# A causal mask moved from the matrix engine to the vector engine, in one attention step of a decoder block

## The chip, the core and the metric

The kernel runs on one core of one Trainium2 chip. The metric is the device time of one execution in microseconds (us); lower is better. The core's engines work from lists of their own: PE multiplies matrices (PEld is its loading of weights), DVE is the vector engine, ACT the scalar engine, POOL does a little, and SP issues transfers. Each engine takes its list strictly in order; semaphores make an instruction wait for other engines.

## What is computed

One decoder layer on 512 tokens of width 1024: a half-step SwiGLU, a mixer (attention with 8 heads of 64 in three branches, beside a state-space part), a second SwiGLU, an embedding gate and a norm. Of the attention only the row statistics of two branches matter here. Selection keeps all eight blocks of 64 keys and the window is 512, so both branches see every earlier key, and their scores are plain causal ones:

```python
s = jnp.einsum('bqghd,bsgd->bghqs', qc, k_w).astype(jnp.float32) * scale
p_win = masked_softmax(s, wmask)            # wmask: key position <= query position
...
def masked_softmax(s, mask):
    s = jnp.where(mask, s, NEG)             # NEG = -1e30
    m = jnp.max(s, axis=-1, keepdims=True)
    e = jnp.where(mask, jnp.exp(s - m), 0.0)
    return e / jnp.maximum(jnp.sum(e, axis=-1, keepdims=True), 1e-30)
```

## The kernel before

The two SwiGLU blocks and the projections are long rows of matrix products: fp32 values are split into a high and a low part (hi, lo), and each product is three matmuls. All matmuls are issued by the helper at line 133, so the profile tells them apart by tile names. The mixer lies in the middle of the run, between about 400 and 600 us.

In the mixer, queries are taken in four blocks of 128 rows (qb = 0 to 3). For every block, `scores(qb)` makes row scores with queries on the partitions and the first nk = 128(qb+1) keys along the free axis. Each step of its loop fills one bank of PSUM (`s_`, named ps_A, ps_B or ps_C by its tag; each tag has two banks that take turns): a matmul of QA with KA, one of QB with KB (the split parts), and a third matmul that adds the mask. That third one multiplies `identb`, an identity in bf16, by `maskq`, a 128x128 table of 0 and -1e30 in bf16, and accumulates onto the last 128 columns, where the diagonal is. Then DVE takes the row maximum (`nmax`, line 1261), and ACT the exponential with its row sum (line 918, in place in the bank). When the exponential has read the bank, the next score with that tag but one may start.

For qb = 2 and 3 a step holds one head and one branch (384 or 512 columns), so there are 16 steps for each of the two blocks, 32 in all. For qb = 0 and 1 a bank holds several heads, and there are 12 further steps.

The text `PLAN` (line 1590) gives the program order of the mixer's pieces: `t3` is a step of scores(3), `t2` of scores(2). Around them run the projections (ps_A from xh, xl with hi, lo), the state-space part (`s5_in`: DVE makes t, vv and z from ps_C; `s5_out`: PE multiplies u8 and z with so into ps_D), two gelu steps (lines 924 and 926 on DVE, with ACT between), the splits of the queries QA (line 1240) and the windows of the compressed branch (`windows`, line 1127: DVE adds cst, which a transfer brings, to pe and writes cs, cosr and sinr; a cst tile must be free of a gelu's `gt` before its transfer starts). The order on each engine is not the program order: line 1746 asks for a schedule by a simulated timeline when the program is built, so a change of one instruction can move others.

## Time and profile before

| | us |
|---|---|
| three runs: lowest, median, highest | 1045.18, 1047.27, 1047.62 |
| the profiled execution, its own time | 1044.96 |
| its span in the trace | 1043.2 |
| PE busy in the span | 1030.2 |
| DVE busy | 824.5 |
| ACT busy | 501.9 |

The profiled execution is 2.3 us below the median of the three runs; 1.8 us of its time lie outside the span. In a timeline row the first number is the start in the span, the second the duration; an "[idle before <-releaser]" at the end says how long the engine had been idle and what ended that. Durations of matmuls overlap, because the engine starts one before the last has drained; the step from one start to the next is what a matmul costs. Row groups ("x20") give busy time and the mean of one in ns.

### The profile page before, as it was taken

To read this page: it belongs to the slowest core of one execution; us is meant where nothing else is said; L and a number is where in the kernel's file an instruction comes from. 1 tells how busy PE (TensorE), PEld (TensorE's weight loads), DVE (VectorE), ACT (ScalarE), POOL (GpSimd) and SP (SyncE) were. 2 spreads that over 40 slices of the span, in tenths; PEclk is the share of its full clock that TensorE was granted. 3 is DMA by queue.
4 is the path that set the end of the run, shared out by engine and by line. 5 is a ranking of instruction groups with operands and counts; after the bars stand their busy time and mean duration, and the time that the engine had idled before them with its cause. 6 is when DMAs were issued, how large, how long until landed. Compare 5 with 4: busy or idle time off the path is not lost.

```text
span 1043.2 us, 15725 instructions
## 1 busy us (share of the span) xinstructions
PE 1030.2 (99%) x6057; PEld 875.7 (84%) x6057; DVE 824.5 (79%) x1382; ACT 501.9 (48%) x868; POOL 159.2 (15%) x180
## 2 busy tenths in 40 slices
PE   9999999999999999999999999999999999999997
PEld 6888888889889888776586688998899899899886
DVE  6798468988989766896688887996598588687666
ACT  6322232535336542476768855653365245245452
POOL 0003948207870200100000000000000000000001
PEclk9999999999999999999999999999999999999999
DMA  7434325636354748766410013433233333333412
GB/s 266 142 87 134 98 88 169 229 121 127 120 135 149 231 118 230 216 193 183 158 41 21 21 61 123 135 107 122 85 98 122 101 102 101 101 102 101 141 61 81
DMA packets 52394, 131.00 MB, mean 126 GB/s; under 512 B 10784, under 2 KB 19072, under 8 KB 52320
## 3 DMA queue, kind: packets, MB, share of 16 engines
q10 hardware_dynamic: 26352, 90.77, 27.3%
q0 software_dynamic: 5872, 17.93, 6.9%
q1 hardware_dynamic: 20096, 21.31, 6.5%
q8 instruction: 47, 0.77, 0.3%
q14 instruction: 27, 0.22, 0.1%
HBM read 114.09 MB, written 15.73 MB: 124 GB/s over the span
## 4 chain that ended last, share of the span: by engine, by line
PE 84%; DVE 5%; DMA 3%; POOL 3%; ACT 2%; issue 2%; SPq 0%; DVEq 0%; ACTq 0%; POOLq 0%
PE ps_A L133 25%; PE ps_C L133 24%; PE ps_B L133 20%; PE ps_D L133 15%; POOL ft L721 1%; POOL bt L720 1%; DMA kf<-kd 1%; DVE lo L166 1%; ACT e L918 1%; DMA kd<-r 1%; DVE el L1360 0%; DMA qf<-qd 0%; DMA h<-in_xT 0%; POOL ft L719 0%; POOL seen L559 0%
## 5 line engine op out<-in xcount | busy, mean ns | idle before, releaser
L164 ACT CAST hi<-raw 128x1024 fp32r<-128x1024 f32 (+2 forms) x143 | 144.4, 1010 | 250.3 <-PE ps_C L133 96.8
L133 PE MATMUL ps_C<-hq,hi 128*128 128x512 f32 x704 | 217.5, 390 | 0.2
L166 DVE TENSOR_TENSOR lo<-raw,hi 128x1024 fp32r<-128x1024 f32 (+2 forms) x143 | 174.2, 1219 | 40.6 <-ACT hi L164 39.9
L133 PEld LDWEIGHTS ps_C<-hq,hi 128*128 128x128 f32 x704 | 130.9, 188 | 28.1 <-DVE h L526 1.3
L133 PE MATMUL ps_C<-hq,lo 128*128 128x512 f32 x352 | 136.9, 389 | 0.0
L133 PE MATMUL ps_A<-xh,hi 128*128 128x512 f32 (+1 forms) x352 | 124.9, 355 | 0.5 <-ACT hi L164 0.5
L133 PE MATMUL ps_A<-xl,hi 128*128 128x512 f32 (+1 forms) x352 | 124.0, 352 | 0.1
L133 PE MATMUL ps_A<-xh,lo 128*128 128x512 f32 (+1 forms) x352 | 122.5, 351 | 0.2 <-DVE lo L166 0.2
L164 ACT CAST hi<-s 128x1024 fp32r<-128x1024 f32 x56 | 58.9, 1052 | 107.0 <-PE ps_D L133 60.9
L166 DVE TENSOR_TENSOR lo<-s,hi 128x1024 fp32r<-128x1024 f32 x56 | 70.7, 1262 | 19.9 <-ACT hi L164 19.7
L133 PEld LDWEIGHTS ps_C<-hq,lo 128*128 128x128 f32 x352 | 66.1, 188 | 13.8
L133 PEld LDWEIGHTS ps_A<-xh,hi 128*128 128x128 f32 x352 | 66.6, 189 | 10.2 <-ACT hi L164 0.7
L133 PEld LDWEIGHTS ps_A<-xh,lo 128*128 128x128 f32 x352 | 66.7, 189 | 9.5 <-DVE lo L166 0.6
L133 PEld LDWEIGHTS ps_A<-xl,hi 128*128 128x128 f32 x352 | 66.5, 189 | 9.7 <-DVE xl L192 0.8
L526 DVE SCALAR_TENSOR_TENSOR h<-ps_C,h 128x512 f32<-128x512 f32 x64 | 43.9, 687 | 36.6 <-PE ps_C L133 36.5
L133 PE MATMUL ps_B<-sh,lo 128*128 128x256 f32 x224 | 63.1, 282 | 0.3 <-DVE lo L166 0.3
L133 PE MATMUL ps_D<-sl,hi 128*128 128x256 f32 x224 | 63.1, 282 | 0.0
L133 PE MATMUL ps_B<-sh,hi 128*128 128x256 f32 x224 | 63.0, 281 | 0.0
L133 PE MATMUL ps_B<-sl,hi 128*128 128x256 f32 x224 | 62.9, 281 | 0.0
L133 PE MATMUL ps_D<-sh,hi 128*128 128x256 f32 x224 | 62.8, 280 | 0.0
L133 PE MATMUL ps_B<-xh,hi 128*128 128x512 f32 (+1 forms) x168 | 62.8, 374 | 0.0
L133 PE MATMUL ps_D<-sh,lo 128*128 128x256 f32 x224 | 62.6, 280 | 0.0
(440 smaller groups left out, 2474.4 us busy)
## 6 DMA issues: line engine op xcount, KB each, us to landing
raw<-in_wpack ACTq DMA_DIRECT2D x168, 512.0 KB, 3.5
si<-s5i POOLq DMA_DIRECT2D x8, 512.0 KB, 5.3
so<-s5o POOLq DMA_DIRECT2D x8, 512.0 KB, 5.6
h<-in_xT SPq DMA_DIRECT2D x8, 256.0 KB, 4.5
s5i<-fs POOLq DMA_DIRECT2D x1, 2048.0 KB, 11.5
xraw<-in_xT SPq DMA_DIRECT2D x8, 256.0 KB, 3.8
s5o<-gt POOLq DMA_DIRECT2D x1, 2048.0 KB, 13.4
s5i<-tcs POOLq DMA_DIRECT2D x2, 1024.0 KB, 10.4
```

Source lines behind the costliest of these rows:

```text
L133: return PE.matmul(o, lhsT, rhs, start=start, stop=stop, **kw)
L164: p, q = S.copy(hi[:, c], raw[:, c]), None
L166: q = V.tensor_tensor(lo[:, c], raw[:, c], hi[:, c].bitcast(F32), OP.subtract)
L526: V.scalar_tensor_tensor(h[:, m, :], o[m], 0.5, h[:, m, :], OP.mult, OP.add)
L720: G.tensor_tensor(bt, b2[:, 1], bc(psn[:, e]), OP.mult)
L721: G.tensor_tensor(ft[:, :, s_, :], ft[:, :, s_, :], bt, OP.add)
L918: S.activation(*args, **kw)
```

## The change

For the last two query blocks the third matmul goes. The matmul of QB with KB ends the accumulation, and DVE adds `maskq` (bf16) to the last 128 columns of the bank in place. For the first two blocks nothing changes.

```diff
-                    mm(s_[:, i], QB[0:112, h0 + i], KBg[0:112, g, rs, :nk], False, False)
-                mm(s_[:, :, :, nk - 128:], identb, maskq[:, None, None, :].to_broadcast([128, n, nb, 128]), False, True)
+                    mm(s_[:, i], QB[0:112, h0 + i], KBg[0:112, g, rs, :nk], False, qb > 1)
+                if qb > 1:
+                    V.tensor_tensor(s_[:, 0, 0, nk - 128:], s_[:, 0, 0, nk - 128:], maskq, OP.add)
+                else:
+                    mm(s_[:, :, :, nk - 128:], identb, maskq[:, None, None, :].to_broadcast([128, n, nb, 128]),
+                       False, True)
```

On PE 32 of the 44 mask matmuls go, with their weight loads; DVE gets 32 adds of 128x128. In the changed kernel the add has line 1260 and the maximum line 1265. The schedule also changes between the first score of qb = 3 and the first products of the attention's values, in the trace of before from 436 to about 555 us; outside that stretch the lists agree. Three places follow. A number behind a tile's name marks one buffer; "[waits Activation_49]" is a wait for ACT, DVE_49 for DVE, PE_49 for PE and DMA... for a transfer.

Place 1, PE, the third and fourth score of qb = 3 (ps_B_4315 and ps_B_4361). Before:

```order
L133 MATMUL ps_B_4315<-KA_3600,QA_4104 128x512 [waits Activation_49]
L133 MATMUL ps_B_4315<-KB_3601,QB_4105 128x512
L133 LDWEIGHTS identb_94
L133 MATMUL ps_B_4315<-maskq_3607,identb_94 128x128
L133 MATMUL ps_A_4327<-xh_3422,hi_4323 128x512
L133 MATMUL ps_A_4327<-xl_3423,hi_4323 128x512
L133 MATMUL ps_A_4327<-xh_3422,lo_4324 128x512
L133 MATMUL ps_B_4361<-KA_3600,QA_4104 128x512 [waits Activation_49]
```

PE in the changed kernel, the same two scores:

```order
L133 MATMUL ps_B_4315<-KA_3600,QA_4104 128x512 [waits PE_49,Activation_49]
L133 MATMUL ps_B_4315<-KB_3601,QB_4105 128x512
L133 MATMUL ps_A_4327<-xh_3422,hi_4323 128x512
L133 MATMUL ps_A_4327<-xl_3423,hi_4323 128x512
L133 MATMUL ps_A_4327<-xh_3422,lo_4324 128x512
L133 MATMUL ps_D_4368<-so_4192,u8_3639 64x128 [waits DMASW3_49,PE_49]
L133 MATMUL ps_D_4368<-so_4192,u8_3639 64x128
L133 MATMUL ps_D_4368<-so_4192,z_3640 64x128
L133 MATMUL ps_B_4361<-KA_3600,QA_4104 128x512 [waits Activation_49]
```

The masks are gone and three short products of the state-space part have come ahead of the fourth score. On ACT, not shown, the second exponential now stands behind a gelu's square (gt from yt), which was behind it before.

Place 2, DVE, ahead of the instruction that makes z_3641 for the state-space part. Before:

```order
L1261 TENSOR_REDUCE nmax_3644<-ps_B_4501 128x1 [waits PE_49]
L166 TENSOR_TENSOR lo_4617<-raw_4614,hi_4616 128x560 [waits Activation_49]
L1127 TENSOR_TENSOR cs_4654<-cst_4659,pe_3619 128x8x32 [waits DMAHW7_49,DMAHW6_49]
L1127 TENSOR_TENSOR cs_4655<-cst_4659,pe_3619 128x8x32
L990 SCALAR_TENSOR_TENSOR vv_4461<-r8_121,t1_4455 128x64 [waits DVE_49]
L990 SCALAR_TENSOR_TENSOR vv_4461<-r8_121,t1_4455 128x64 x3
L1261 TENSOR_REDUCE nmax_3644<-ps_B_4507 128x1 [waits PE_49]
L1261 TENSOR_REDUCE nmax_3644<-ps_C_4574 128x1 [waits PE_49]
L994 TENSOR_TENSOR z_3641<-vv_4461,si_4446 128x8x63 [waits DVE_49]
```

DVE in the changed kernel, up to the same z_3641:

```order
L1260 TENSOR_TENSOR ps_C_4574<-ps_C_4574,maskq_3607 128x128 [waits PE_49]
L1265 TENSOR_REDUCE nmax_3644<-ps_B_4501 128x1 [waits DVE_49]
L990 SCALAR_TENSOR_TENSOR vv_4461<-r8_121,t1_4455 128x64 [waits DVE_49]
L990 SCALAR_TENSOR_TENSOR vv_4461<-r8_121,t1_4455 128x64 x3
L1265 TENSOR_REDUCE nmax_3644<-ps_C_4574 128x1 [waits DVE_49]
L1240 SCALAR_TENSOR_TENSOR QA_4785<-qf_4788,QA_4785 64x512 [waits DMAHW1_49,Activation_49]
L1260 TENSOR_TENSOR ps_B_4507<-ps_B_4507,maskq_3607 128x128 [waits PE_49]
L924 SCALAR_TENSOR_TENSOR gt_4591<-gt_4591,yt_4438 128x512 [waits Activation_49]
L994 TENSOR_TENSOR z_3641<-vv_4461,si_4446 128x8x63 [waits DVE_49]
```

A query split (L1240) and a gelu step (L924) have come ahead of z, and eight adds stand ahead of it in all. PE's first product with z_3641 has moved back too: 20 more products of the value projection (ps_A, 280 wide) stand ahead of it than before.

Place 3, DVE, the second pair of cs, which needs a transfer into cst. Before:

```order
L1261 TENSOR_REDUCE nmax_3644<-ps_B_4537 128x1 [waits PE_49]
L926 SCALAR_TENSOR_TENSOR yt_4438<-gt_4591,yt_4438 128x512 [waits Activation_49]
L1108 SCALAR_TENSOR_TENSOR VL_3602<-ps_A_4620,ri_3686,VL_3602 128x4x64 [waits Activation_49]
L1110 TENSOR_SCALAR gp1_3606<-ps_A_4620,ri_3686 128x24
L1261 TENSOR_REDUCE nmax_3644<-ps_B_4585 128x1 [waits PE_49]
L1127 TENSOR_TENSOR cs_4654<-cst_4656,pe_3619 128x8x32 [waits DMAHW5_49,DMAHW4_49]
```

DVE in the changed kernel:

```order
L926 SCALAR_TENSOR_TENSOR yt_4438<-gt_4591,yt_4438 128x512 [waits Activation_49]
L1108 SCALAR_TENSOR_TENSOR VL_3602<-ps_A_4620,ri_3686,VL_3602 128x4x64 [waits Activation_49]
L1110 TENSOR_SCALAR gp1_3606<-ps_A_4620,ri_3686 128x24
L1240 SCALAR_TENSOR_TENSOR QA_4785<-qf_4818,QA_4785 64x512 [waits DMAHW7_49,Activation_49]
L1265 TENSOR_REDUCE nmax_3644<-ps_B_4531 128x1 [waits DVE_49]
L1260 TENSOR_TENSOR ps_B_4537<-ps_B_4537,maskq_3607 128x128 [waits PE_49,Activation_49]
L1127 TENSOR_TENSOR cs_4654<-cst_4656,pe_3619 128x8x32 [waits DMAHW3_49,DMAHW2_49]
L1127 TENSOR_TENSOR cs_4655<-cst_4656,pe_3619 128x8x32
L1265 TENSOR_REDUCE nmax_3644<-ps_B_4537 128x1 [waits DVE_49]
```

The maximum of score ps_B_4537 has moved from ahead of the gelu's last step (L926) to behind the pair that waits for the transfer. On SP that transfer now stands ahead of two transfers of queries that were ahead of it.

## The prediction

> **What bounds the kernel now.** I read the page's first part and the chain that ended last, then the stretches around the change, then PE's waits there.

> ```profile
> span 1043.2 us, 15725 instructions
> PE 1030.2 (99%) x6057; PEld 875.7 (84%) x6057; DVE 824.5 (79%) x1382; ACT 501.9 (48%) x868; POOL 159.2 (15%) x180
> PE 84%; DVE 5%; DMA 3%; POOL 3%; ACT 2%; issue 2%; SPq 0%; DVEq 0%; ACTq 0%; POOLq 0%
> ```

> PE sets the time: it idles only 13 us of the span. So a matmul taken away is worth its step, unless PE then waits. Whether it waits is read in the stretch of the 32 scores; columns are busy time (and count) of PE, PEld, DVE, ACT, POOL, then PE's clock, DMA share and GB/s:

> ```profile
> 434.00:442.00 8.00, 8.00 (x56) 5.82 (x55) 7.38 (x16) 3.70 (x7) 1.85 (x3) 1.00 0.76 225
> 442.00:470.00 28.00, 26.72 (x205) 20.14 (x203) 27.36 (x56) 20.98 (x45) 1.51 (x2) 1.00 0.64 199
> 470.00:484.00 14.00, 12.88 (x95) 10.15 (x95) 10.23 (x20) 10.84 (x26) 1.17 (x2) 1.00 0.46 113
> 484.00:524.00 40.00, 40.00 (x220) 24.77 (x216) 26.85 (x53) 26.84 (x71) 0.00 (x0) 1.00 0.54 181
> ```

> From 442 to 470 DVE is as full as PE (27.36 of 28 us against 26.72); from 470 on it has 3.8 us to spare, and from 484 another 13. The change takes work from the engine that bounds and gives it to one that for 28 us has no room. PE's waits from 430 to 525, and the masks:

> ```profile
> PE ps_B L133 <- ACT ps_B L918: 1.2, 1, 1.2
> PE ps_A L133 <- DVE cosr L1127: 0.7, 1, 0.7
> PE ps_A L133 <- PE ps_A L133: 0.4, 1, 0.4
> L133 PE MATMUL ps_B<-maskq,identb 128*128 128x128 bf16 x20 | 4.6, 231 | 0.0
> L133 PE MATMUL ps_C<-maskq,identb x12: 230/231/234, 460.5 to 521.7; 128*128 128x128 bf16 x12
> ```

> The first wait is for a score's exponential, the second for DVE's cosr. 20 and 12 masks of this form are the 32 that go.

> **Taken from PE.** A mask's 231 ns overlap its neighbours; its cost is in the steps between starts:

> ```profile
> 458.85 0.39 PE L133 MATMUL ps_B<-KA,QA 128*128 128x512 f32 x1
> 459.08 0.39 PE L133 MATMUL ps_B<-KB,QB 112*128 112x512 f32 x1
> 459.31 0.23 PE L133 MATMUL ps_B<-maskq,identb 128*128 128x128 bf16 x1
> 459.35 0.48 PE L133 MATMUL ps_C<-KA,QA 128*128 128x512 f32 x1
> 459.66 0.40 PE L133 MATMUL ps_B<-KA,QA 128*128 128x512 f32 x1
> ```

> Without a mask the step is 0.23 (458.85 to 459.08). With it, 459.31 to 459.66 holds the mask and one matmul: 0.35, so the mask costs 0.12. Bounds: 0.04, if only its own step (459.31 to 459.35) goes, and 0.23, if its whole duration goes. I take 0.12, since the longer step behind a mask recurs: 32 x 0.12 = 3.8 us. Against the span and the profiled 1044.96 this is the gross gain; ends 1.3 and 7.4.

> [...]

> **Given to DVE.** No add of 128 columns in PSUM is in the trace. The nearest rows are the same shape in SBUF, and 256 columns from PSUM:

> ```profile
> L660 DVE TENSOR_TENSOR u<-pi 128x128 f32<-128x128 f32 x1 | 0.3, 286 | 0.0
> L1280 DVE TENSOR_TENSOR ec<-ps_B,ec 128x256 f32<-128x256 f32 x4 | 1.7, 421 | 0.6 <-ACT ec L1279 0.6
> ```

> So 0.29, upper end 0.42. Durations overlap the next one a little:

> ```profile
> 441.79 0.68 DVE L1261 TENSOR_REDUCE nmax<-ps_B 128x1 f32<-128x512 f32 x1
> ...
> 455.25 0.42 DVE L984 TENSOR_TENSOR t<-ps_C,si 128x256 f32<-128x256 f32 x1
> 455.68 0.42 DVE L985 TENSOR_TENSOR t<-ps_C,si 64x256 f32<-64x256 f32 x1
> ...
> 466.42 0.68 DVE L1261 TENSOR_REDUCE nmax<-ps_C 128x1 f32<-128x512 f32 x1
> 467.02 0.68 DVE L994 TENSOR_TENSOR z<-vv,si 128x504 f32<-128x504 f32 x1
> ```

> A step of 0.60 for a duration of 0.68 where the next operation needs nothing of this one: an add takes 0.21 to 0.29 of the queue; I use 0.25, and 32 of them are 8 us. What matters is which PE wait they move. I counted DVE's new list forward from 441.79, the first maximum of before, with these steps: 0.60 to 0.70 for 512 columns, 0.43 for 256 (455.25 to 455.68).

> **Where the gain goes, up to cosr.** The first two masks stand ahead of a PE wait that ACT sets:

> ```profile
> 444.61 0.66 ACT L918 ACTIVATE ps_B<-ps_B,nmax 128x512 f32<-128x512 f32 x1
> 445.28 0.65 ACT L918 ACTIVATE ps_B<-ps_B,nmax 128x512 f32<-128x512 f32 x1
> 445.44 0.50 PE L133 MATMUL ps_B<-KA,QA 128*128 128x512 f32 x1 [1.18 <-ACT ps_B L918]
> 446.84 0.40 PE L133 MATMUL ps_B<-KA,QA 128*128 128x512 f32 x1
> 446.86 0.63 ACT L918 ACTIVATE gt<-yt 128x512 f32<-128x512 f32 x1 [0.81 <-DMA qd<-r]
> ```

> The third score starts 0.83 behind the first exponential (444.61 to 445.44), and ACT is what is late; 0.24 is lost. At place 1 the second exponential now stands behind the gelu's square, which waits for a transfer (446.86 in before; some 0.7 earlier now, because two adds, not two maxima, stand ahead of the sum that is transferred): it starts near 446.65 instead of 445.28, and the fourth score near 447.5 instead of 446.84. PE is there near 446.9: lost 0.6.

> The eighth score (ps_B_4507) waits for the fifth exponential, which in before came right behind its maximum:

> ```profile
> 456.57 0.69 DVE L1261 TENSOR_REDUCE nmax<-ps_B 128x1 f32<-128x512 f32 x1
> 457.36 0.66 ACT L918 ACTIVATE ps_B<-ps_B,nmax 128x512 f32<-128x512 f32 x1 [2.10 <-DVE nmax L1261]
> ```

> In the new DVE list that maximum has five adds ahead of it (1.25) and a query split, a gelu step, a scan and z that were behind it (4.2): it starts near 462.1, the exponential near 462.8, the score near 463.6, and PE is there near 462.3: lost 1.3.

> z_3641 itself comes 2.8 later (eight adds 2.0, split and gelu 1.3, a maximum fewer 0.6), near 469.8 instead of 467.02. In before PE waited a little for it:

> ```profile
> 467.24 0.29 PE L133 MATMUL ps_A<-hi,xl 128*128 128x280 f32 x1
> 467.36 0.29 PE L133 MATMUL ps_A<-hi,xh 128*128 128x280 f32 x1
> 467.75 0.44 PE L133 MATMUL ps_D<-so,z 128*64 128x128 f32 x4
> ```

> The 20 products that now stand ahead of it cover 20 x 0.12 (467.24 to 467.36) = 2.4, and PE itself is later by the losses (2.1) less ten masks (1.2): no wait, and the 0.25 of before is won.

> Next is the chain from the gelu's last step over two transfers into cst to cosr, on which the compression products wait (DVE, SP, PE):

> ```profile
> 473.53 0.69 DVE L926 SCALAR_TENSOR_TENSOR yt<-gt,yt 128x512 f32<-128x512 f32 x1
> 474.64 0.49 SPq L1120 DMA_DIRECT2D cst<-kcd  x1
> 478.13 1.12 DVE L1127 TENSOR_TENSOR cs<-cst,pe 128x256 f32<-128x256 f32 x2 [2.77 <-DMA cst<-kcd]
> 482.60 0.58 DVE L1127 TENSOR_TENSOR cosr<-cst,pe 128x256 f32<-128x256 f32 x1 [0.30 <-DMA cst<-vcd]
> 483.24 0.43 PE L133 MATMUL ps_A<-raw,cosr 128*64 128x256 f32 x1 [0.68 <-DVE cosr L1127]
> ```

> My count puts L926 at 473.1 in spite of ten adds, since the gelu's first step was brought forward, and SP no longer holds the transfer back behind the queries' (474.64 stands 0.4 behind L926's end). So cs starts near 477.3 and the cosr product near 482.4, 0.8 earlier. But two 384-wide scores (two steps of at most 0.23 each, so some 0.9 in all) that PE had done ahead of it now come behind. Net at this point: 0. The 17 masks gone by here (2.0 us) have paid for new waits. At place 3 one is plain: the maximum of ps_B_4537 stands behind cs, and the score that needs its bank behind that, so PE waits 1.4 there instead of 1.1 at two later places.

> **Behind cosr** 15 masks go, 15 x 0.12 = 1.8, beside a DVE with 13 us of slack; for the longer chain of each score (add, then maximum) and the new order up to 555 I take back 0.5. Sum: -1.3 us: profiled 1043.7 instead of 1044.96, and as the median of runs, which lies 2.3 above the profiled time, 1047.27 - 1.3 = 1046.0. A measurement of this kernel can tell about 0.3%, 3.1 us, from no change.

> **Rivals.** *All hidden:* PE's waits stay as they were, the gain is the gross 3.8 and the time 1043.4; with 0.16 a mask it is 5.1 and 1042.2. For it: the reordering puts 20 products ahead of z, and DVE is free from 470 on. Against: the full stretch 442 to 470.

> *Slower, by the turn of the score banks:* ps_B carries most scores of qb = 3, two banks in turn, and PE in its order stops at a score whose bank is not read. Each bank now passes an add and, in DVE's order, what stands between add and maximum. If each of nine scores from the fourth on waits 0.9 (between my 0.6 and 1.3), PE loses 8.1, nets +4.3 and ends at 1051.6. It decides for slower when new waits exceed 3.8 + 3.1 = 6.9. For it: the [2.10] above, where ACT already waited for a maximum; against: the scheduler moved other products ahead of the scores, and in before PE waited for a bank once. [...]

> *It thins nothing:* the new waits equal the gross gain over the whole stretch, not only up to cosr, and the time stays at 1047.3. This lies inside the forecast's range.

> **Numbers.** Chances: the forecast with its edge, so within 0.3%, 0.62; all hidden, faster by over 0.3%, 0.21; slower by over 0.3%, 0.17. The forecast's own range is 1044.2 to 1049.0 (add at 0.42 instead of 0.25: ten adds ahead of L926, +1.7; a mask at 0.04: +2.6). For 8 in 10 I go to 1042.5, the gross gain with dearer masks, and up to 1050.5, part of the slower case.

> **What would show it.** Right: 32 adds of 0.25 to 0.3 us at line 1260; PE's busy time down by 2 to 4 us and its idle time up by 2 or more between 442 and 484, on ACT's line 918; cosr's product starting 482 to 483; from 484 to 524 no new PE wait over 0.5. Wrong: if PE's waits from 442 to 484 stay at 2.3 (all hidden) or pass 7 (slower); if an add takes over 0.42; or if the lists up to 555 bring a wait I did not count.

## The result, and the profile after

The changed kernel takes 1054.3 us (median of 6 runs, 1052.92 to 1056.36) against 1046.8 of the kernel before (6 runs, 1045.18 to 1047.62): ratio 1.0073, 95% interval 1.0062 to 1.0084. It is slower by about 7.6 us, where 1046.0 with a range of 1042.5 to 1050.5 was forecast. Its profiled execution is the slowest of the six, so the profile shows some 2 us more than the median. One of the twelve runs of p3 below took 1448.4 us at a granted clock of 0.655, and p3's ratio is that of the other eleven.

The page of the changed kernel, first and fourth part:

```profile
span 1054.6 us, 15711 instructions
PE 1033.8 (98%) x6025; PEld 879.7 (83%) x6025; DVE 830.8 (79%) x1414; ACT 502.2 (48%) x868; POOL 159.5 (15%) x180
PE 82%; DVE 6%; DMA 4%; POOL 3%; issue 2%; ACT 2%; SPq 0%; DVEq 0%; ACTq 0%; POOLq 0%
```

PE has 32 matmuls fewer and is busy 3.6 us longer. The stretches say why; columns as before, the last but two is PE's granted clock:

```profile
434.00:442.00 8.00, 7.85 (x53) 5.82 (x52) 7.74 (x18) 3.97 (x8) 1.86 (x3) 1.00 0.74 221
442.00:470.00 28.00, 24.88 (x142) 19.11 (x140) 23.27 (x51) 16.68 (x34) 1.51 (x2) 0.82 0.51 161
470.00:484.00 14.00, 14.00 (x115) 12.04 (x116) 11.12 (x26) 9.40 (x23) 1.17 (x2) 1.00 0.67 165
484.00:524.00 40.00, 35.71 (x172) 21.13 (x170) 28.31 (x64) 25.88 (x63) 0.00 (x0) 0.96 0.57 178
524.00:560.00 36.00, 34.73 (x202) 29.08 (x200) 31.51 (x76) 24.29 (x81) 0.00 (x0) 1.00 0.16 47
```

From 434 to 560 PE idles 8.8 us, in the kernel before 2.6. Besides, its clock falls: 0.82 over 28 us and 0.96 over 40 are 5.0 and 1.6 us of full clock. DVE, which was full from 442 to 470 (27.36 of 28), is idle for 4.7 us there. PE's waits from 430 to 525 (total, times, longest):

```profile
PE ps_B L133 <- ACT ps_B L918: 3.3, 3, 2.2
PE ps_A L133 <- DMA raw<-in_wpack: 3.2, 2, 1.8
PE ps_A L133 <- DVE cosr L1127: 0.9, 1, 0.9
```

and the adds, from the view of the tile maskq (shortest, median and longest in ns):

```profile
L1260 DVE TENSOR_TENSOR ps_B<-ps_B,maskq x20: 277/292/300, 441.6 to 529.4; 128x128 f32<-128x128 f32 x20
L1260 DVE TENSOR_TENSOR ps_C<-ps_C,maskq x12: 277/288/300, 469.7 to 531.1; 128x128 f32<-128x128 f32 x12
```

An add takes 0.29 us, as forecast. Place 1, from the timeline of SP, ACT and PE:

```profile
443.35 0.33 SPq L1058 DMA_DIRECT2D qd<-r  x1
444.46 0.66 ACT L918 ACTIVATE ps_B<-ps_B,nmax 128x512 f32<-128x512 f32 x1
448.21 0.63 ACT L918 ACTIVATE gt<-yt 128x512 f32<-128x512 f32 x1 [2.96 <-DMA qd<-r]
448.74 0.64 ACT L918 ACTIVATE ps_B<-ps_B,nmax 128x512 f32<-128x512 f32 x1
449.56 0.50 PE L133 MATMUL ps_B<-KA,QA 128*128 128x512 f32 x1 [2.23 <-ACT ps_B L918]
```

The square stands between the exponentials, as the order said. But the transfer, issued 0.95 earlier than before (443.35, not 444.30), landed near 448.2 instead of 446.8, and the fourth score starts at 449.56. The clock behind it, by stretches of 4 us:

```profile
446.00:450.00 4.00, 1.77 (x12) 0.96 (x10) 1.43 (x5) 1.70 (x4) 0.00 (x0) 1.00 0.41 158
450.00:454.00 4.00, 4.00 (x32) 3.33 (x32) 3.89 (x9) 3.93 (x9) 0.76 (x1) 0.63 0.27 74
454.00:458.00 4.00, 4.00 (x20) 3.38 (x19) 3.94 (x7) 2.49 (x5) 0.00 (x0) 0.50 0.54 158
458.00:462.00 4.00, 4.00 (x12) 3.13 (x11) 3.85 (x10) 0.78 (x2) 0.00 (x0) 0.59 0.45 166
462.00:466.00 4.00, 4.00 (x28) 2.65 (x27) 2.35 (x7) 1.42 (x4) 0.75 (x1) 1.00 0.42 131
```

and two matmuls there, from the timeline:

```profile
457.50 0.63 PE L133 MATMUL ps_A<-xh,lo 128*128 128x512 f32 x1
457.92 0.63 PE L133 MATMUL ps_A<-xh,hi 128*128 128x512 f32 x1
```

After a stretch in which PE works 1.77 of 4 us the clock is at half for 10.2 us, and a 512-wide product takes a step of 0.42 instead of 0.23. Later on, from the timeline of DVE, SP, ACT and PE:

```profile
476.84 0.68 DVE L926 SCALAR_TENSOR_TENSOR yt<-gt,yt 128x512 f32<-128x512 f32 x1
477.59 0.47 SPq L1120 DMA_DIRECT2D cst<-kcd  x1
482.53 1.08 DVE L1127 TENSOR_TENSOR cs<-cst,pe 128x256 f32<-128x256 f32 x2 [1.88 <-DMA cst<-kcd]
487.62 0.43 PE L133 MATMUL ps_A<-raw,cosr 128*64 128x256 f32 x1 [0.88 <-DVE cosr L1127]
...
497.55 0.63 ACT L1238 ACTIVATE QA<-qf 128x512 fp32r<-128x512 f32 x1 [4.67 <-DMA qf<-qd]
499.64 0.43 PE L133 MATMUL ps_A<-raw,cs 128*63 128x256 f32 x1 [1.39 <-DMA raw<-in_wpack]
501.23 0.34 ACTq L107 DMA_DIRECT2D raw<-in_wpack  x1
504.92 0.67 PE L133 MATMUL ps_A<-yt,raw 128*128 128x512 f32 x1 [1.77 <-DMA raw<-in_wpack]
559.97 0.50 PE L133 MATMUL ps_D<-eh,VLc 128*128 128x512 f32 x1 [1.22 <-ACT eh L918]
```

cosr's product comes 4.4 us later than in the kernel before (483.24). Behind it ACT stands 4.67 us before a query copy, and the next weight loads in its queue (from 501.23) stand behind that. PE waits 1.77 us for the first of these and 1.22 us for eh, the high part of the attention's exponentials. Its wait of 1.39 us for raw at 499.64 is for a load that was issued ahead of that copy, by 491.7. So there are three suspects: the adds on DVE, single places of the new order (place 1 and its fallen clock, the loads), and the new order as a whole.

### The profile page after: what moved, and what is told of

Read it like the earlier page. It is cut to its first block, busy times and chain, and to the rows that moved or that the text cites. A ratio compares the mean times of both kernels' runs of the same rounds, so it can differ in the third digit from the quotient of the medians.

```text
span 1054.6 us, 15711 instructions
## 1 busy us (share of the span) xinstructions
PE 1033.8 (98%) x6025; PEld 879.7 (83%) x6025; DVE 830.8 (79%) x1414; ACT 502.2 (48%) x868; POOL 159.5 (15%) x180
## 4 chain that ended last, share of the span: by engine, by line
PE 82%; DVE 6%; DMA 4%; POOL 3%; issue 2%; ACT 2%; SPq 0%; DVEq 0%; ACTq 0%; POOLq 0%
PE ps_A L133 24%; PE ps_C L133 23%; PE ps_B L133 19%; PE ps_D L133 15%; DMA qf<-qd 1%; POOL ft L721 1%; DVE lo L166 1%; POOL bt L720 1%; DMA qd<-r 1%; DMA raw<-in_wpack 1%; DVE el L1364 1%; DMA cst<-kcd 0%; DVE s L342 0%; POOL ft L719 0%; DVE nmax L1265 0%
## 5 line engine op out<-in xcount | busy, mean ns | idle before, releaser
L133 PE MATMUL ps_C<-hq,hi 128*128 128x512 f32 x704 | 217.6, 391 | 0.4 <-DVE h L526 0.2
L133 PEld LDWEIGHTS ps_C<-hq,hi 128*128 128x128 f32 x704 | 130.8, 188 | 28.5 <-DVE h L526 1.9
L133 PE MATMUL ps_C<-hq,lo 128*128 128x512 f32 x352 | 136.8, 389 | 0.0
L133 PE MATMUL ps_A<-xh,hi 128*128 128x512 f32 (+1 forms) x352 | 125.2, 356 | 1.1 <-ACT xh L191 0.7
L133 PE MATMUL ps_A<-xl,hi 128*128 128x512 f32 (+1 forms) x352 | 124.8, 355 | 0.3 <-DVE xl L192 0.3
L133 PE MATMUL ps_A<-xh,lo 128*128 128x512 f32 (+1 forms) x352 | 123.2, 353 | 0.2 <-DVE lo L166 0.2
L133 PEld LDWEIGHTS ps_C<-hq,lo 128*128 128x128 f32 x352 | 66.1, 188 | 13.9
L133 PEld LDWEIGHTS ps_A<-xh,hi 128*128 128x128 f32 x352 | 67.0, 190 | 11.3 <-ACT xh L191 1.2
L133 PEld LDWEIGHTS ps_A<-xh,lo 128*128 128x128 f32 x352 | 67.1, 191 | 9.7 <-DVE lo L166 0.6
L133 PEld LDWEIGHTS ps_A<-xl,hi 128*128 128x128 f32 x352 | 67.0, 190 | 9.8 <-DVE xl L192 0.6
L133 PE MATMUL ps_B<-sh,lo 128*128 128x256 f32 x224 | 63.1, 282 | 0.3 <-DVE lo L166 0.3
L133 PE MATMUL ps_D<-sl,hi 128*128 128x256 f32 x224 | 63.1, 282 | 0.0
L133 PE MATMUL ps_B<-sh,hi 128*128 128x256 f32 x224 | 63.0, 281 | 0.0
L133 PE MATMUL ps_B<-sl,hi 128*128 128x256 f32 x224 | 62.9, 281 | 0.0
L133 PE MATMUL ps_D<-sh,hi 128*128 128x256 f32 x224 | 62.8, 280 | 0.0
L133 PE MATMUL ps_B<-xh,hi 128*128 128x512 f32 (+1 forms) x168 | 62.7, 374 | 0.0
L133 PE MATMUL ps_D<-sh,lo 128*128 128x256 f32 x224 | 62.6, 280 | 0.0
```

Source lines behind the costliest of these rows:

```text
L133: return PE.matmul(o, lhsT, rhs, start=start, stop=stop, **kw)
```

## Experiments

All ratios are to the kernel before on the same chip, with 95% interval; 0.1% is 1.05 us.

**Parts of the change.** The add for one block alone, no mask at all (the mask of qb = 2 and 3 is left out), and products with adds of zeros beside them. In these four the scheduler makes its own order each time.

```diff
-  False, qb > 1)  /  if qb > 1: V.tensor_tensor(...)
+  False, qb == 2) /  if qb == 2: V.tensor_tensor(...)    # e3; e4: qb == 3
-  V.tensor_tensor(s_..., maskq, OP.add)
+  pass                                                   # e5
+  if qb > 1: V.tensor_tensor(s_..., zero..., OP.add)     # e6, in the kernel before
```

> The add for the 16 scores of qb = 2, the mask product kept for the 16 of qb = 3. ACT has its two exponentials ahead of the gelu's square, as before. Theory A: no loss at place 1, ratio 0.997 to 1.001 (16 masks of 0.12 are 1.9 us of gain at most). Theory B, by the number of adds: half the loss, ratio 1.003 to 1.005.

> The add for the 16 scores of qb = 3, the product kept for qb = 2. ACT has the gelu's square between the first and the second exponential, as in the changed kernel. Theory A: nearly the whole loss, ratio 1.005 to 1.009, with a PE wait of 2 to 4 us for the second exponential and a clock below 0.9 from 442 to 470. Theory B, by the number of adds: half, ratio 1.003 to 1.005; by where DVE is full (442 to 470): also nearly the whole loss, but as many waits of about 1 us, at a clock of 1.00.

> No mask at all for qb = 2 and 3: neither product nor add. ACT's order at place 1 is that of before. All theories: the gross gain of the 32 products, 32 x 0.12 = 3.8 us, ratio 0.9963; by 0.081 each 2.6 us, 0.9975. Theory B: that with DVE as free as before nothing of it is lost. If it comes out at 1.000 or above, then taking the products away brings nothing even without the adds, because PE waits there for something else.

> The kernel before, mask products kept, with an add of zeros on VectorE of the same shape behind each of the 32: PE's work as before, DVE's and the scores' chain as in the changed kernel. ACT has the gelu's square between the first two exponentials, as in the changed kernel. If what costs is the adds on DVE (their time and the order that they make): the whole loss and no gain, ratio 1.007 to 1.012, with a clock drop behind place 1. If what costs is that PE has less work and so arrives early: ratio 1.000 to 1.004, since PE's work is that of before.

Measured: e3 1.0010 (1.0001 to 1.0020), e4 1.0068 (1.0051 to 1.0085), e5 0.9995 (0.9984 to 1.0007), e6 1.0062 (1.0043 to 1.0081). The loss goes with the 16 adds of qb = 3 and with the order in which the square splits the exponentials (e4, e6). It doesn't need PE's lighter work (e6). And leaving the products out, with nothing in their place, brought nothing clear of noise (e5). Adds and order still go together in all four.

**Place 1 undone, three ways.** e1 makes the first square issue behind the second exponential. e8 and e9 give the gelu other buffers, so that it does not wait for the transfer.

```diff
+  with tc.issue_after(exps[1]): act(t, x, AF.Square)     # e1, first gelu only
-GT = "r1", "r2"
+GT = "r3", "r2"                                          # e8;  e9: "rb1", "r3"
```

> All 32 adds stay; only the first gelu square is made to issue behind the second exponential of the qb = 3 scores, as it did in the kernel before. Theory A (the loss is that one order on ACT: a 3 to 4 us PE wait, the granted clock that falls behind it, and what comes late after it): PE is busy over 25.5 of 28 us from 442 to 470, the clock of that stretch is 0.97 or more, and the time comes back by 5 to 9 us, ratio to the kernel before 0.997 to 1.002. Theory B (DVE's 8 us of adds and the longer turn of each score bank): the wait only moves, ratio 1.005 to 1.009. Theory C (ACT's weight loads that come late at 498 to 506 us): half is left, ratio 1.002 to 1.005, and PE still waits over 2 us for raw.

> The changed kernel, with the first gelu's gt in the buffer tag r3 instead of r1, so that its square does not wait for the transfer qd<-r. ACT now has the square ahead of both exponentials, which follow each other. If the wait on the transfer is what costs: PE waits for exponentials 1.5 us or less at place 1, no clock drop from 448 to 462, ratio 1.000 to 1.004; if the adds on DVE cost wherever the square stands: 1.005 to 1.009.

> As the last, with both gelu tags changed (rb1 and r3), so that no gelu shares a buffer with what is transferred. ACT has the two exponentials first, then the square. Place 1 as in the kernel before; what is left is the load on DVE and the later waits (cosr, raw): ratio 1.000 to 1.005. Above 1.005 the wait on the transfer was not needed for the loss.

Measured: e1 1.0044 (1.0028 to 1.0060), e8 1.0042 (1.0029 to 1.0054), e9 1.0045 (1.0032 to 1.0059). About 3 us of 7.6 come back each time. In e8 cosr's product is at 483.15, as early as in the kernel before, and the loss lies behind it, where PE waits for loads among other things:

```profile
494.73 0.43 PE L133 MATMUL ps_A<-raw,cs 128*63 128x256 f32 x1 [1.01 <-DMA raw<-in_wpack]
500.27 4.94 PE L133 MATMUL ps_A<-yt,raw 128*128 128x512 f32 x7 [1.83 <-DMA raw<-in_wpack]
```

My first theory, that place 1 is the loss, was then too narrow, and it had been tested with edits that re-ordered the rest.

**The clock.** e7 fills the wait at place 1 with useless products.

```diff
+  [mm(o[0:64], KAc[:, 128:192], nm.xh[:, k, :], False, False) for _ in range(9)]   # kc, last k
```

> The changed kernel, with nine products more by a block of zeros (64 columns of KAc that stay zero, x 512, 0.23 us each, 2.1 us) in the kc projection, which stand on PE just ahead of the fourth score, in its wait of 2.2 us; ACT's order at place 1 stays. They do no useful work, so that PE is busy where it waited, and nothing comes earlier. If the fallen clock behind the wait is what costs there (4.8 us of clock time from 451 to 462): PE's wait for the second exponential under 0.5, clock 1.00 from 448 to 462, and faster than the changed kernel by 3 to 5 us, ratio 1.002 to 1.004 to the kernel before. If the wait alone costs, and the clock only shows it: no change or slower, ratio 1.007 to 1.010.

Measured: 1.0073 (1.0061 to 1.0086), no change. The filler did what it should, by stretches:

```profile
446.00:450.00 4.00, 3.32 (x14) 1.80 (x12) 1.53 (x6) 1.87 (x5) 0.00 (x0) 1.00 0.25 97
450.00:454.00 4.00, 3.30 (x37) 2.57 (x36) 3.92 (x8) 2.67 (x7) 0.76 (x1) 1.00 0.36 80
```

and by PE's timeline:

```profile
445.78 2.23 PE L133 MATMUL ps_A<-xh,KAc 128*64 128x512 f32 x9
449.39 0.50 PE L133 MATMUL ps_B<-KA,QA 128*128 128x512 f32 x1 [0.68 <-ACT ps_B L918]
470.35 0.44 PE L133 MATMUL ps_D<-so,u 128*64 128x128 f32 x4 [1.37 <-ACT yt L1023]
```

The clock stays at 1.00 through the whole stretch of e7's profile, and PE, faster there, waits at other places instead (1.37 for yt, 10.7 us of idle time from 430 to 620 against 9.5). My expectation of 3 to 5 us was wrong. But the scheduler re-ordered the stretch in e7 too (PE's list and DVE's differ from those of the changed kernel far beyond the filler), so e7 alone does not show what the fallen clock costs. The loss does not need it, though: p4 below, whose profile has one fall of 3.4 us (1.7 us of full clock), loses 10.9 us.

**The loads.** raw from GpSimd's queue: in the changed kernel (e10), with e8's buffer (e11), in the kernel before (e12), and with the add for qb = 3 alone (e13).

```diff
-  raw = unit(True, at=next(at["cmp"]))        # and "glu"
+  raw = unit(True, q=G, at=next(at["cmp"]))
```

> The changed kernel, with the weights of the compression and of the gated unit (raw) loaded from GpSimd's queue instead of ACT's, where they stand behind a copy that waits 4.7 us for the queries (qf<-qd). The scheduler then puts the two exponentials ahead of the gelu's square again. If that wait on ACT's queue is the second cause: PE waits for raw under 0.5 in 484 to 524 (3.2 in the changed kernel), ratio 1.002 to 1.005. If the adds on DVE cost all by themselves, ratio 1.005 to 1.009 and the wait is for something else.

> Both: raw from GpSimd's queue, and the first gelu's gt in r3, so that no square waits for qd<-r. If the two blocked waits on ACT are all of the loss, ratio 0.997 to 1.001; if the adds on a full DVE are a part of it that no order takes away, 1.002 to 1.004.

> The kernel before, mask products kept, with raw from GpSimd's queue. No PE wait for raw stands in its profile: no change, ratio 0.999 to 1.001. It is the measure for the last two.

> As the run with both, but the add for qb = 3 alone and the product kept for qb = 2. If the adds of qb = 3, which lie where DVE is full (442 to 484), are what costs: the same ratio as with all 32 adds, within 0.1%, or above. If each add costs alike: half of it. PE's wait of 1.2 for eh near 555 should be gone, as in the run with the add for qb = 3 alone.

Measured: e10 1.0101 (1.0080 to 1.0122), e11 1.0048 (1.0032 to 1.0064), e12 1.0048 (1.0033 to 1.0063), e13 1.0044 (1.0026 to 1.0061). The measure itself moved: e12, which differs from the kernel before by the queue of these loads and the order that the scheduler then makes, is 5 us slower. Like the kernel before it has no wait for raw, but PE's waits from 430 to 525 are these:

```profile
PE ps_B L133 <- ACT ps_B L918: 3.6, 3, 2.1
PE ps_D L133 <- ACT yt L1023: 1.6, 1, 1.6
PE ps_A L133 <- DVE cosr L1127: 0.5, 1, 0.5
```

So these four say nothing on the loads, but they gave the next theory: a re-ordered stretch can cost 5 us and more, whatever re-orders it.

**Work and order apart.** In the next kernels every engine's order is fixed by a table. p1 is the changed kernel in the order of the kernel before: the products left out of PE's list, each add right ahead of its maximum. p2 has no mask (left out, as in e5) and p3 products and adds of zeros, both in that order. p4 is the kernel before in the order of the changed kernel.

```diff
     block_kernel(tc, aps, out)
+    pin(tc)    # for each engine, each instruction of ORDER behind the one ahead of it, no wait
```

> The changed kernel's instructions in the order of the kernel before on every engine: its 32 products left out of PE's list, each add right ahead of its maximum in DVE's; ACT, GpSimd and SP word for word as before. If the new order is what costs: ratio 0.997 to 1.001, gelu's square behind both exponentials, PE's wait for cosr 0.7 to 3, clock 1.00. If the adds themselves cost (DVE full from 442 to 470, ten adds of 0.20 to 0.25 us ahead of cosr): cosr's product 2 us later than in the kernel before and ratio 1.002 to 1.006.

> No mask for qb = 2 and 3, neither product nor add, in the order of the kernel before. The pure worth of the 32 products: 3.8 us at 0.12 each, ratio 0.9963, or 2.6 us at 0.081, 0.9975; less where PE only waits more (cosr and the exponential, up to 2 us): 0.998 to 0.999. In the scheduler's own order it was 0.9995.

> Products kept, and an add of zeros of the same shape ahead of each of the 32 maxima, in the order of the kernel before. The pure price of the adds on DVE: if the order is what costs, ratio 1.000 to 1.002; if DVE's time is (32 x 0.20 to 0.25 us, 6.4 to 8), 1.003 to 1.008. In the scheduler's own order it was 1.0062.

> The kernel before, products and no adds, in the order of the changed kernel on every engine (each product right behind its score's second one). The pure price of the order: if it is the order, ratio 1.004 to 1.009, with the square of the gelu between the exponentials, its wait for qd<-r and a clock drop; if it is the adds, 0.999 to 1.003.

| work | old order | new order |
|---|---|---|
| products (before) | 1 | p4: 1.0104 (1.0087 to 1.0121) |
| adds (the change) | p1: 1.0015 (1.0004 to 1.0026) | 1.0073 (1.0062 to 1.0084) |
| neither | p2: 0.9988 (0.9979 to 0.9997) | |
| both | p3: 1.0025 (1.0016 to 1.0034) | |

This settles whether it is the work or the order. With the order kept, the change costs 1.6 us; the other 6.1 of its 7.6 come with the new order (1.0073 against 1.0015; the steps are rounded). With the work kept, the new order costs 10.9 us, and in that order the adds are 3.2 us better than the products (1.0073 against 1.0104). p1, p3 and p4 came out a little above the ranges that I had given for an order that costs all (1.001, 1.002 and 1.009 at most). No run has the table on a kernel's own order, with nothing changed; p5 below is the changed kernel with its own order in the table but for one step, and its 1.0071, against 1.0073, shows no price of the table itself. The stretches of p1, p2 and p4, in this order, three rows each:

```profile
442.00:470.00 28.00, 24.64 (x183) 19.40 (x182) 27.20 (x60) 19.04 (x41) 1.51 (x2) 1.00 0.58 195
470.00:484.00 14.00, 12.13 (x90) 9.97 (x88) 11.27 (x24) 10.85 (x26) 1.17 (x2) 1.00 0.48 118
484.00:524.00 40.00, 38.72 (x190) 23.96 (x191) 31.23 (x68) 26.55 (x68) 0.00 (x0) 0.96 0.59 190
```

```profile
442.00:470.00 28.00, 25.59 (x191) 20.21 (x189) 26.40 (x55) 20.15 (x42) 1.51 (x2) 1.00 0.62 204
470.00:484.00 14.00, 12.75 (x89) 10.33 (x87) 10.22 (x19) 11.69 (x30) 1.17 (x2) 1.00 0.50 119
484.00:524.00 40.00, 39.15 (x209) 25.53 (x209) 28.10 (x55) 26.79 (x71) 0.00 (x0) 1.00 0.57 185
```

```profile
442.00:470.00 28.00, 25.62 (x186) 19.07 (x185) 23.59 (x50) 17.62 (x36) 1.51 (x2) 1.00 0.58 177
470.00:484.00 14.00, 12.40 (x96) 9.99 (x95) 10.12 (x21) 8.84 (x24) 1.17 (x2) 1.00 0.60 157
484.00:524.00 40.00, 34.88 (x173) 19.88 (x174) 23.68 (x44) 24.91 (x62) 0.00 (x0) 0.96 0.56 177
```

PE's idle time in these rows is 2.4 us in the kernel before, 4.5 in p2, 6.5 in p1 and 9.1 in p4. p2 shows what the products are worth: over the whole span PE is busy 3.2 us less than in the kernel before (1027.0 against 1030.2). In these rows 2.1 us of new waits eat most of that, and by the ratio 1.25 are left (0.3 to 2.2 by its interval). In p4 no add is on DVE, which is idle for 4.4 us from 442 to 470, and PE waits 8.2 us for exponentials (up to 4.1 for one) all the same.

**Which place of the new order.** p5 is the changed kernel in its own order but for the second exponential, ahead of the square; p6 also has two loads ahead of the query copy on which ACT stands.

```diff
 ACT's list:
-exp 1, square, exp 2 ...   QA<-qf, ... raw, ... raw
+exp 1, exp 2, square ...   QA<-qf, ... raw, ... raw      # p5
+exp 1, exp 2, square ...   raw, raw, QA<-qf, ...         # p6
```

> The changed kernel in its own order on every engine, but for one step on ACT: the second exponential ahead of the gelu's square at place 1. If place 1 carries most of the price: PE's fourth score starts 2 to 3 us earlier, the clock stays at 1.00 from 448 to 462, and 3 to 6 us come back, ratio 1.002 to 1.0045. If PE then only waits elsewhere: 1.006 to 1.008.

> As the last, and two loads of raw weights on ACT's queue ahead of the query copy (QA<-qf) that waits 4.7 us for its transfer. If those loads carry the rest: PE's waits for raw fall from 3.2 to under 1.5 us and another 1 to 3 us come back, ratio 1.000 to 1.003. If the next wait takes its place (a score's exponential, or cosr): the same ratio as the last within 0.1%.

Measured: p5 1.0071 (1.0057 to 1.0085), p6 1.0079 (1.0065 to 1.0093). Neither gives anything back. Both steps do what they should: in p5 the fourth score starts at 447.44, in p6 no PE wait for raw is left. The next wait takes the place each time; PE's timeline of p5:

```profile
447.44 0.50 PE L133 MATMUL ps_B<-KA,QA 128*128 128x512 f32 x1
484.90 0.50 PE L133 MATMUL ps_B<-KA,QA 128*128 128x512 f32 x1 [2.21 <-ACT ps_B L918]
```

and of p6:

```profile
501.36 0.69 PE L133 MATMUL ps_B<-KA,QA 128*128 128x384 f32 x1 [2.80 <-ACT ps_B L918]
```

cosr's product stays at 487.30 and 486.89 (487.62 in the changed kernel). So no one of the places that I named carries the price of the order.

Two products tell in which part of the stretch it lies: cosr's first, and the first of the attention's values (eh with VLc). The first row is the kernel before (cosr's is at 483.24 there), the other two are p1:

```profile
549.66 0.39 PE L133 MATMUL ps_D<-eh,VLc 128*128 128x512 f32 x1
487.04 0.69 PE L133 MATMUL ps_A<-raw,cosr 128*64 128x256 f32 x1 [1.06 <-DVE cosr L1127]
553.54 0.39 PE L133 MATMUL ps_D<-eh,VLc 128*128 128x512 f32 x1
```

From the one to the other it is 66.4 us in the kernel before and 66.5 in p1 and p3, but 72.4 in the changed kernel, 74.3 in p4, 71.6 in p5 and 72.8 in p6. PE idles at most 0.1 us there in the old order and 4.1 to 5.4 in the new one, which also has two scores more in it (four steps of at most 0.23, so some 0.9 us, as an estimate).

Up to cosr's product the profiles do not tell the orders apart: p1 and p3, with adds in the old order, are as late (487.04 and 487.34) as the changed kernel (487.62) and p4 (486.70). These are single executions, and p1's is 3.9 us longer than that of the kernel before, where the ratio says 1.6. So most of what only the new order costs lies behind cosr's product. Which property of the order makes PE wait there is open: when the waits for raw went (p6), waits for exponentials stood in their place. No kernel tried is faster than the one before by more than p2, which lacks the mask; the version to keep is the one before.

## Why the prediction was wrong, by its steps

The step that failed is the pricing of the new order. The prediction followed it only at a few places up to cosr's product and gave all that stands behind them 0.5 us. Of the 7.6 us the new order makes 6.1 (the change against p1), and with the old work it alone costs 10.9 (p4), of which 7.9 lie behind cosr's product in p4's profile. The work alone, adds for products, costs 1.6 us (p1), where the whole change was forecast at -1.3. Why the order costs so much is not known further than the waits shown above.

- **Bounds.** Right: PE had no room, and DVE none from 442 to 470.
- **Taken from PE, 3.8 us gross.** The size was nearly right: 3.2 by p2's busy time, so 0.10 a mask instead of 0.12. The 0.081 a mask that the expectations of e5 and p2 name is shown by no run; what the runs show in its place is this 0.10. But I took off only the first two masks and a few later waits, and named the rest a gain. With nothing added anywhere 2.1 us of it become waits: in this stretch PE's work covers the others' time.
- **Given to DVE.** The add was right (0.29, step 0.20: the one at 441.64 is followed at 441.84). Its price was not 8 us but 2.6 (p3 against 1) to 2.8 (p1 against p2); my counts had put about 2.5 on the path. As a price of the work alone the forecast of -1.3 missed by 2.9: p1 is at +1.6. That time, about 1048.4, lies within the range.
- **Place 1, 0.6 us. This is the first step that failed.** I let the transfer land as long behind its issue as before, near 446.1, and it landed near 448.2, so that the score came at 449.56, not 447.5. When I then took this for the cause, that failed too: p5 has the score at 447.44 and no gain.
- **Eighth score, 1.3 us.** Not there in the changed kernel, where PE runs at half clock until 461.3. With the full clock, in p5, PE waits 0.39 and 1.24 for exponentials at 460.60 and 465.57: of the size forecast.
- **z.** No wait of PE for it in the changed kernel, as forecast.
- **L926, cs and cosr, net 0. Failed.** L926 was forecast at 473.1 and came at 476.84, cs at 477.3 and came at 482.53, cosr's product at 482.4 and came at 487.62. I counted DVE's list forward as if it never waited; it idles 4.7 us from 442 to 470, 2.57 of them for the square. Yet that is not the only way to be late: in p1, where DVE idles 0.8 us in that time, L926 starts at 476.93 and cosr's product at 487.04.
- **Behind cosr, -1.8 + 0.5. The largest miss.** There the profile loses another 6 us to the loads, a second fall of the clock and eh (the first product with eh of VLc lies 10.3 us behind that of the kernel before, cosr's product 4.4). I allowed 0.5 for an order up to 555 that I had not followed there.
- **The range.** Its ends, 1044.2 and 1049.0, do not follow from the two terms beside them: +1.7 and +2.6 on 1046.0 make 1050.3. The wider range, up to 1050.5, covers that, and the result lies above both.
- **The rivals.** That it is slower had 0.17, by nine short waits for score banks. The sign came, not that way: PE waits three times for exponentials in 430 to 525. A rival that the new order costs more than the work, whatever the work, was not among mine, though the order had been shown to me from 436 to 555.
- **What would show it.** PE's busy time did not fall by 2 to 4 us, it rose by 3.6 at a lower clock; the clock was no part of my forecast.

## What to carry to other kernels

Where a scheduler re-orders a stretch, a small edit has two prices, the work's and the order's, and the second can be several times the first (here 6.1 with the new work and 10.9 with the old, against 1.6 us): run the new work in the old order before blaming an instruction. An edit that takes one wait away is no test of that wait if the stretch is re-ordered by it; hold every other instruction in place. And products taken from the engine that bounds are worth only what its neighbours can follow (in p2 3.2 us of PE's busy time went, and 1.25 of the time): ask what the next release is before counting their time as gain.

## What the runs showed of the hardware

A transfer of one tile (qd<-r) took 4.9 us from issue to the operation that waits for it (443.35 to 448.21), and about 2.6 in the kernel before (444.30 to 446.86), beside the same loads (the DMA engines' busy share in the 2-us stretches from 442 and 444 was 0.95 and 0.84, before 1.01 and 0.98). Issuing it 0.95 us earlier did not bring it earlier.
